# Attention fillers by a fixed count per head instead of a round robin

## The chip, the cores and the metric

The kernel runs on one core of one Trainium2 chip. The metric is the device time of one execution in microseconds (us), taken as the median of several runs. A core has a matrix engine (TensorE, PE in the profile, with PEld for its weight loads), a vector engine (VectorE, DVE), an activation engine (ScalarE, ACT), a general engine (GpSimd, POOL) and a queue that issues the transfers (SyncE, SP). Each engine takes its own instructions strictly in the order in which they stand in the program, and waits for the others on semaphores.

## The reference, cut to what matters

One inference step of two layers on 512 prompt tokens and 8 samples of 4 new tokens each, 544 token columns in all, model width 1024, in fp32. Layer 0 is RWKV-7 time mixing. Layer 1 is native sparse attention (NSA) with 16 query heads on 4 key/value heads:

```python
q, kc, vc, ks, vs, kw, vw, z, gl = jnp.split(h @ w_in, cuts, axis=-1)
...
o = g[..., 0:1] * o_c + g[..., 1:2] * o_s + g[..., 2:3] * o_w    # compressed, selected, window branch
...
return (o.reshape(B, T, NSA_QDIM) * jax.nn.silu(z)) @ w_o
```

So layer 1 is an input projection (28 blocks of 128 output channels), three attention branches for the prompt, the same for the samples against their caches, a gate by silu(z), and an output projection with a residual. The outputs are the new activations, the new key and value rows and the recurrent state.

## The kernel before, in words

Layer 0 is not touched. Layer 1 (`layer1`) is written as Python generators, each of which issues instructions up to its next `yield`; the code at the end of `layer1` decides in what order they are advanced.

* `dense(...)` (`jobs`) does the 28 input projections. One job multiplies a 128-channel weight block, split in two parts for fp32 accuracy, with all 544 columns: 48 matmuls of 128x272 (line 325), 24 into each of two PSUM banks. It yields 8 times, so one dense step is 6 matmuls. In the middle of the next job it does the follow-up of the last one (`post`): head norms (lines 1506 to 1516), key, value and query rows, or the silu of z.
* `attend(k)` goes through the four blocks of 128 queries of key/value head k, in the order of `BO`. A block is done in two halves m (two query heads each). A half computes scores on PE (line 1725), adds the bias table and takes the row maximum on DVE (1752), exponentiates on ACT (1759) and scales the probabilities on DVE or POOL (1779). `attend` yields four times per block, 16 times per head. At each step it also advances the value generator of the block before (`self.pending`): PE transposes (1803), copies from PSUM by ACT (1806) or DVE (1808), value products (1816, 1819), an eviction on ACT (1821) and a store to the DRAM tensor dO (1826). `flush()` advances the values of a head's last block and has four steps of its own.
* `attend_sample(i)` does the samples for the heads 2i and 2i+1, with 32 yields: cache loads and scores (1876, 1884), evictions with bias (1881 to 1892), a softmax (DVE 1896 to 1906, ACT 1901, POOL 1909), transposes (1917 to 1922) and value products (1930 to 1950).
* `gated` loads the stored attention output and silu(z) of six 128-channel blocks, multiplies them (1999) and splits each product into two operands (286 on ACT, 287 on DVE); `project_out` (`part`) multiplies these with the output weights, 48 steps of 6 matmuls (325 again). `project_last` adds the two blocks of head 3 (2041).

Dense jobs, sample steps and the output projection are called fillers: `together(main, filler, n)` advances the filler n times after every step of the attention, and `mix` takes one step from each of its fillers in turn. `until(...)` advances the dense jobs alone until given results exist. All these matmuls share the 3 one-bank PSUM buffers `ph` (a projection takes two at a time, a sample step one); scores and transposes use 2 two-bank buffers `pq`.

The order so written isn't the final one. A scheduler places the instructions of each engine by an estimate of when they can start, with the written order as their priority; it can lift a later matmul over one that it thinks would wait. The code before:

```python
until(("kc", 0), ("ks", 0), ("kw", 0), ("q", 0), ("q", 1))
together(attend(0), jobs, PLAN["N"][0])                  # N = (3, 4, 4, 4)
until(("q", 3), *kv(0))
sample = attend_sample(0)
together(attend(1), mix(jobs, sample), PLAN["N"][1])
until(*kv(1), ("q", 7))
```

Of the kernel before, what the change touches and what calls it, by code (L numbers as in the profile page):

```python
# [2 lines left out]

# [22 lines left out]
PLAN = {  # L26
    'F0': 8,
    'ZN': 7,
    'UN': 7,
    'FN': 3,  # L30
    'LAG': 2,
    'SN': 3,
    'FS': 5,
    'VS': (0, 0, 1, 1, 1, 1, 1, 3),
# [15 lines left out]
    'DS': 4,  # L50
    'BO': ((3, 0, 2, 1), (0, 2, 3, 1), (3, 2, 0, 1), (3, 2, 0, 1)),
    'JO': [('kc', 0), ('ks', 0), ('q', 0), ('kw', 0), ('q', 1), ('vs', 0), ('vc', 0), ('vw', 0), ('kc', 1), ('vc', 1), ('q', 2), ('q', 3), ('ks', 1), ('kw', 1), ('q', 4), ('q', 5), ('vs', 1), ('vw', 1), ('q', 6), ('q', 7), ('z', 0), ('z', 1), ('z', 2), ('z', 3), ('z', 4), ('z', 5), ('z', 6), ('z', 7)],
    'N': (3, 4, 4, 4),
    'PT': 1,
    'PO': 2,
    'PW': 1,
# [17 lines left out]
NR = 32  # L74
F0, ZN, UN, FN, LAG, SN, FS, VS, IV = (PLAN["F0"], PLAN["ZN"], PLAN["UN"], PLAN["FN"], PLAN["LAG"], PLAN["SN"], PLAN["FS"], PLAN["VS"], PLAN["IV"])
TW = 528

VECS = ["nw0", "nw1", "mr", "mw", "mk", "mv", "ma", "mg", "w0", "a0", "kk", "ka", "rk", "lw", "lb"]
VI = {n: i for i, n in enumerate(VECS)}
# [144 lines left out]
class K:  # L224
# [1297 lines left out]
    def layer1(self):  # L1522
# [178 lines left out]
        def kv(i):  # L1701
            return [(n, i) for n in ("kc", "vc", "ks", "vs", "kw", "vw")]

        def bias_tables(k):
            t = self.t("tb", (128, 4, TW))
            for a in range(0, 128, NR):
# [121 lines left out]
        def attend(k):  # L1828

            order = PLAN["BO"][k]  # L1830
            for n, b in enumerate(order):
                if (k, b) not in QZ:
                    stacked_queries(k, b)
                s, v = scores(k, b), self.pending
                next(s)
                if b != order[-1]:
                    stacked_queries(k, order[n + 1])
                next(v, None)
                yield
                for _ in s:  # L1840
                    next(v, None)
                    yield
                for _ in v:
                    yield
                self.pending = values(k, b)
# [3 lines left out]
        def flush():  # L1849
            yield from self.pending  # L1850
            self.pending = iter(())
# [116 lines left out]
        jobs = dense(PLAN["JO"])  # L1968

        def until(*names):  # L1970
            while not ready.issuperset(names):
                next(jobs)

        def together(main, filler, n):
            for _ in main:
                for _ in range(n):
                    next(filler, None)

        def project_out(ks, src, dst):

# [61 lines left out]
                        nc.vector.tensor_tensor(x[:, a], pt[a][:, :HN], x[:, a], OP.add)  # L2042
                    nc.sync.dma_start(O["y"][:, m:m + 2, c], x)

        def mix(*fillers):

            fillers = list(fillers)
            while fillers:
                for f in list(fillers):
                    if next(f, f) is f:  # L2050
                        fillers.remove(f)
                    else:
                        yield

        until(("kc", 0), ("ks", 0), ("kw", 0), ("q", 0), ("q", 1))
        together(attend(0), jobs, PLAN["N"][0])
        until(("q", 3), *kv(0))
        sample = attend_sample(0)
        together(attend(1), mix(jobs, sample), PLAN["N"][1])
        until(*kv(1), ("q", 7))  # L2060
        for _ in sample:
            pass
        sample = attend_sample(1)
        together(attend(2), mix(jobs, sample), PLAN["N"][2])
        together(flush(), mix(jobs, sample), PLAN["N"][2])
        for _ in jobs:
            pass
        for _ in sample:
# [1 line left out]
        gated(range(6))  # L2070
        gate_last()
        part = project_out(range(6), self.dx1, dx2)
        together(attend(3), part, PLAN["N"][3])
        together(flush(), part, PLAN["N"][3])
        for _ in part:
            pass
        project_last()
# [52 lines left out]
```

## Time and profile before

| what | value |
|---|---|
| median of 3 runs | 1046.39 us (1042.59 to 1049.2) |
| the profiled execution's own time | 1041.69 us |
| its span, first to last instruction | 1039.9 us |
| mean granted PE clock | 0.963 of full speed |
| PE busy | 956.3 us, 92% of the span |
| DVE, ACT, POOL busy | 662.8, 566.4, 471.4 us |
| first and last scores of layer 1 (line 1725) | start at 650.2 and 1015.8 us |

In a timeline row stand the start in us, the length in us, the engine, the line, the operation, the tile written and the tile read, and in brackets how long the engine was idle before it and who ended the wait. A stage row gives the stretch, its length, each engine's busy time with its number of instructions, the granted PE clock, the share of the transfer engines and GB/s. Consecutive matmuls overlap, so a row of n matmuls is worth less than n times the mean.

### The profile page before, as it was taken

The page shows a single profiled execution, that of the slowest core. Times are in us where ns is not written, and L with a number is a line of the kernel's source. Part 1 is how long each engine was busy: PE and PEld are TensorE (multiplying, and loading weights), DVE is VectorE, ACT ScalarE, POOL GpSimd, SP SyncE. Part 2 cuts the span into 40 slices and gives each one's busy share as a digit, 9 for nine tenths or more (in the row PEclk, how much of TensorE's full clock was granted, in tenths as well). Part 3 has the DMA queues.
Part 4 walks back from the last instruction along what each step waited for, and adds up shares of the span by engine and source line. Part 5 has one row for each costly group of instructions (what it writes and reads, how often), then busy time and mean ns, then how long its engine had stood idle before and what let it go on. Part 6 is the DMA issues. An engine that isn't in the chain of part 4 may idle for free. (4 is left out here: it accounts for less than half of the span.)

```text
span 1039.9 us, 24788 instructions
## 1 busy us (share of the span) xinstructions
PE 956.3 (92%) x9429; PEld 848.9 (82%) x9429; DVE 662.8 (64%) x1504; ACT 566.4 (54%) x1333; POOL 471.4 (45%) x573
## 2 busy tenths in 40 slices
PE   5799998989989999999898899999799998998997
PEld 4789997979777878888788888998678877896986
DVE  3788578698486542556866724756676557447654
ACT  4357686555444244545544645656675576566452
POOL 5924557755920453312322665755244445244530
PEclk8799999999999999999999989999999998999999
DMA  5685525648654463745684623333435432438543
GB/s 187 198 259 202 166 87 159 195 135 238 195 149 122 139 176 118 225 119 132 155 246 142 228 83 116 104 112 102 113 92 145 120 91 76 129 89 262 168 143 108
DMA packets 151368, 156.69 MB, mean 151 GB/s; under 512 B 53330, under 2 KB 99954, under 8 KB 150994
## 3 DMA queue, kind: packets, MB, share of 16 engines
q1 hardware_dynamic: 151250, 155.11, 50.0%
q8 instruction: 74, 1.21, 0.5%
q14 instruction: 44, 0.36, 0.1%
HBM read 111.33 MB, written 43.93 MB: 149 GB/s over the span
## 5 line engine op out<-in xcount | busy, mean ns | idle before, releaser
L325 PE MATMUL ph<-x,l 128*128 128x272 f32 x2448 | 361.8, 299 | 11.1 <-DVE l L287 2.5
L325 PEld LDWEIGHTS ph<-x,l 128*128 128x128 f32 x2448 | 327.4, 193 | 31.3 <-issue 8.9
L287 POOL TENSOR_TENSOR l<-w,l 128x512 fp32r<-128x512 f32 (+2 forms) x118 | 157.3, 1345 | 128.5 <-ACT l L286 104.8
L286 ACT ACTIVATE l<-w 128x512 fp32r<-128x512 f32 (+2 forms) x160 | 93.9, 613 | 108.5 <-PE ph L325 42.7
L325 PE MATMUL pp<-x,l 128*128 128x272 f32 x768 | 111.8, 300 | 6.0 <-POOL l L287 6.0
L325 PEld LDWEIGHTS pp<-x,l 128*128 128x128 f32 x768 | 104.0, 195 | 8.6 <-POOL l L287 6.2
L1759 ACT ACTIVATE a<-a,st 128x512 f32<-128x512 f32 (+3 forms) x128 | 70.6, 553 | 24.2 <-DVE st L1752 23.8
L1752 DVE CUSTOM_DVE_ANT_0 a<-pq,tb 128x512 f32<-128x512 f32 (+3 forms) x128 | 56.7, 485 | 18.0 <-PE pq L1725 17.8
L1725 PE MATMUL pq<-p,z 128*128 128x512 f32 (+7 forms) x288 | 58.8, 333 | 5.8 <-DVE st L1752 3.2
L1803 PE MATMUL pq<-cst,a 128*128 128x128 f32 x320 | 52.2, 286 | 5.7 <-DVE h L1808 2.9
L1779 DVE TENSOR_SCALAR a<-a,st 128x128 f32<-128x128 f32 (+3 forms) x112 | 56.2, 562 | 0.6
L325 PE MATMUL pp<-t,l 128*128 128x272 f32 x384 | 54.1, 292 | 0.0
L1725 PEld LDWEIGHTS pq<-p,z 128*128 128x128 f32 x288 | 43.4, 193 | 13.1 <-issue 5.1
L325 PEld LDWEIGHTS pp<-t,l 128*128 128x128 f32 x384 | 50.2, 188 | 0.7
L287 POOL TENSOR_TENSOR d<-d,d 128x544 fp32r<-128x544 f32 (+2 forms) x21 | 27.4, 1303 | 51.1 <-ACT d L286 46.7
L1803 PEld LDWEIGHTS pq<-cst,a 128*128 128x128 f32 x320 | 38.4, 145 | 12.7 <-issue 5.0
L1499 DVE TENSOR_TENSOR d<-ph,RS 128x272 f32<-128x272 f32 x56 | 23.9, 436 | 38.7 <-PE ph L325 34.8
L1806 ACT ACTIVATE h<-pq 128x512 f32<-128x512 f32 x60 | 35.3, 589 | 20.9 <-PE pq L1803 19.8
L287 DVE TENSOR_TENSOR l<-w,l 128x512 fp32r<-128x512 f32 x42 | 36.2, 873 | 16.0 <-ACT l L286 14.6
L1819 PE MATMUL pw<-h,p 128*64 128x256 f32 x320 | 40.4, 402 | 2.8 <-ACT h L1806 2.6
L1772 POOL TENSOR_TENSOR cc<-cc,st 128x64 f32<-128x64 f32 x32 | 12.5, 391 | 53.2 <-DVE st L1769 31.2
L666 POOL TENSOR_TENSOR d<-d,d 128x544 f32<-128x544 f32 x8 | 11.0, 1380 | 56.2 <-ACT d L384 56.2
(419 smaller groups left out, 2001.7 us busy)
## 6 DMA issues: line engine op xcount, KB each, us to landing
w<-in_rkvz SPq DMA_DIRECT2D x64, 256.0 KB, 2.8
d<-dram SPq DMA_DIRECT2D x54, 272.0 KB, 3.8
w<-in_win SPq DMA_DIRECT2D x56, 256.0 KB, 3.0
dram<-d SPq DMA_DIRECT2D x48, 272.0 KB, 3.2
ab<-dram SPq DMA_DIRECT2D x32, 256.0 KB, 3.8
p<-in_xT SPq DMA_DIRECT2D x16, 272.0 KB, 3.8
tb<-dram SPq DMA_DIRECT2D x16, 264.0 KB, 7.0
dram<-uar SPq DMA_DIRECT2D x8, 512.0 KB, 3.5
```

Source lines behind the costliest of these rows:

```text
L286: nc.scalar.activation(hi, raw, AF.Copy)
L287: (eng or nc.gpsimd).tensor_tensor(lo, raw, hi.bitcast(F32), OP.subtract)
L325: nc.tensor.matmul((pt[h][:m, :HN] if split else pt[:m, h, :HN]), a[:, k, :m], b[:, h * HN:(h + 1) * HN], start=(k == 0 and n == 0), stop= ...
L1499: self.nc.vector.tensor_tensor(o, p, r, OP.mult)
L1725: nc.tensor.matmul(p[:, par], QZ[k, b][x][:, par, m], kk[:, lo:hi], start=(x == 0), stop=(x == 1))
L1752: nc.vector.tensor_tensor_reduce(out=P[par][j], in0=p[:, par, :n], in1=TB[k][:, g, o:o + n], scale=-1.0, scalar=3.0e38, op0=OP.add, op1=OP ...
L1759: nc.scalar.activation(P[par][j], P[par][j], AF.Exp, scale=-1.0, bias=st[:, 0, g, j + 1:j + 2], accum_out=st[:, 1, g, j + 1:j + 2])
L1772: nc.gpsimd.tensor_tensor(cc[:, gs], cc[:, gs], r[:, :, 0:1].to_broadcast([128, 2, 32]), OP.mult)
L1779: (nc.gpsimd if e == "p" else nc.vector).tensor_scalar(pj, pj, rr, None, op0=OP.mult)
L1803: nc.tensor.transpose(pt[:, g % 2, g // 2], PB[g][j][:, c * 128:c * 128 + 128], ident)
L1806: nc.scalar.activation(w, pt, AF.Copy)
L1819: nc.tensor.matmul(po[r], v, W[x][:, par], start=False, stop=(x == 0), skip_group_check=True)
```

## The change

`mix` and the table `N` go. `paced(main, (filler, total), ...)` advances each filler on its own: after step n of the attention it takes so many steps that total x n / 16 of them (rounded down) are done. A step count of 16 is one head; where `flush` follows in the same chain, its four steps count on at the same rate.

```diff
-        def together(main, filler, n):
+        def paced(main, *fillers):
+
+            n = 0
             for _ in main:
-                for _ in range(n):
-                    next(filler, None)
+                n += 1
+                for f, total in fillers:
+                    for _ in range(total * n // STEPS - total * (n - 1) // STEPS):
+                        next(f, None)
...
         until(("kc", 0), ("ks", 0), ("kw", 0), ("q", 0), ("q", 1))
-        together(attend(0), jobs, PLAN["N"][0])
+        paced(attend(0), (jobs, 56))
         until(("q", 3), *kv(0))
         sample = attend_sample(0)
-        together(attend(1), mix(jobs, sample), PLAN["N"][1])
+        paced(attend(1), (jobs, 48), (sample, 36))
         until(*kv(1), ("q", 7))
         for _ in sample:
             pass
         sample = attend_sample(1)
-        together(attend(2), mix(jobs, sample), PLAN["N"][2])
-        together(flush(), mix(jobs, sample), PLAN["N"][2])
+        paced(chain(attend(2), flush()), (jobs, 60), (sample, 36))
         for _ in jobs:
             pass
...
         part = project_out(range(6), self.dx1, dx2)
-        together(attend(3), part, PLAN["N"][3])
-        together(flush(), part, PLAN["N"][3])
+        paced(chain(attend(3), flush()), (part, 48))
```

In steps of the written order: head 0 takes 56 dense steps instead of 48, head 1 takes 48 instead of 32, head 2 takes all that are left (60 are offered) within its own 16 steps instead of 32 there, 16 beside its flush and the rest alone. The sample steps go from 2 to 2.25 per attention step. The output projection beside head 3 goes from 4 to 3 per step.

The final order on the engines, at three places. Names with numbers are buffers; in the changed file the same statement has another line number (325 is 326, 1725 is 1726, 1803 is 1804, 1816 is 1817, 1819 is 1820, 1876 is 1877; 1999 is 2004, 287 is 288).

First, PE where head 2's first scores (the last of them, 128x32) meet the value products of head 1's last but one block. Before:

```order
L1725 MATMUL pq_1889_11207<-p_1679_9969,z_1884_11188 128x32
L1725 MATMUL pq_1889_11207<-p_1679_9969,z_1885_11189 128x32
L1511 MATMUL ph_1880_11165<-d_1879_11162,mean_480 128x272
L1819 MATMUL pw_1840_10877<-h_1831_10838,p_1526_9062 64x256 x2
L1819 MATMUL pw_1840_10877<-h_1830_10832,p_1526_9062 64x256 x2
L1819 MATMUL pw_1840_10877<-h_1827_10789,p_1526_9062 64x256 x2
L1819 MATMUL pw_1840_10877<-h_1826_10783,p_1526_9062 64x256 x2
```

The same place now:

```order
L1726 MATMUL pq_1889_11207<-p_1659_9857,z_1885_11189 128x32
L326 MATMUL ph_1930_11449<-x_1337_7963,l_1927_11440 128x272
L326 MATMUL ph_1930_11449<-x_1344_7991,l_1926_11439 128x272
L326 MATMUL ph_1930_11449<-x_1345_7992,l_1926_11439 128x272
L326 MATMUL ph_1930_11449<-x_1344_7991,l_1927_11440 128x272
L326 MATMUL ph_1930_11449<-x_1351_8019,l_1926_11439 128x272
L326 MATMUL ph_1930_11449<-x_1352_8020,l_1926_11439 128x272
L326 MATMUL ph_1930_11449<-x_1351_8019,l_1927_11440 128x272
L1877 MATMUL ph_1902_11275<-s_1922_11406,QB1_8192 32x256 x2
L1877 MATMUL ph_1902_11275<-s_1923_11411,QB1_8192 32x256 x2
```

Where one head-norm matmul stood between the scores and the value products, 17 dense matmuls and the samples' scores stand now (ten more dense ones follow these rows, and then the value products).

Second, PE in the flush of head 2, where the last probabilities are transposed (1803). Before, ph is the bank of a dense job:

```order
L325 MATMUL ph_2081_12415<-x_1309_7851,l_2077_12405 128x272
L325 MATMUL ph_2081_12415<-x_1310_7852,l_2077_12405 128x272
L325 MATMUL ph_2081_12415<-x_1309_7851,l_2078_12406 128x272
L1803 MATMUL pq_2063_12286<-cst_63,a_2022_11999 128x128
L1803 MATMUL pq_2063_12286<-cst_63,a_2023_12000 128x128
L1803 MATMUL pq_2063_12286<-cst_63,a_2040_12099 128x128
L1803 MATMUL pq_2063_12286<-cst_63,a_2041_12100 128x128
L325 MATMUL ph_2081_12415<-x_1316_7879,l_2077_12405 128x272
L325 MATMUL ph_2081_12415<-x_1317_7880,l_2077_12405 128x272
L325 MATMUL ph_2081_12415<-x_1316_7879,l_2078_12406 128x272
```

Now (x_2101 and x_2100 are gated operands of the output projection):

```order
L326 MATMUL ph_2147_12709<-x_2101_12513,l_2143_12699 128x272
L326 MATMUL ph_2147_12709<-x_2100_12512,l_2144_12700 128x272
L1804 MATMUL pq_2078_12438<-cst_63,a_2066_12318 128x128
L1804 MATMUL pq_2081_12451<-cst_63,a_2066_12318 128x128
L1804 MATMUL pq_2078_12438<-cst_63,a_2067_12319 128x128
L1817 MATMUL pw_2084_12464<-ct_2077_12436,VM_8196 64x128 x4
L1804 MATMUL pq_2081_12451<-cst_63,a_2067_12319 128x128
L1804 MATMUL pq_2078_12438<-cst_63,a_2047_12197 128x128
L1804 MATMUL pq_2078_12438<-cst_63,a_2048_12198 128x128
```

From the last scores of head 2 to the first of head 3, 123 dense matmuls stood on PE before. Now 33 matmuls of the output projection stand there, and no dense one.

Third, DVE at the gate of the output projection (1999 multiplies, 287 makes the second operand). Before, after the first scores of head 3:

```order
L1752 ISA st_2119_12571 128x1
L1767 TENSOR_SCALAR st_2119_12571<-st_2119_12571 128x6
L1999 TENSOR_TENSOR d_2094_12498<-d_2094_12498,d_2095_12500 128x544
L287 TENSOR_TENSOR x_2089_12486<-d_2086_12480,x_2088_12485 128x544
L1588 TENSOR_TENSOR z_2164_12825<-q_1864_11077,z_2164_12825 64x256 x2
L1746 TENSOR_TENSOR cc_2157_12803<-pq_2158_12804,CB_8198 128x64
```

Now, ahead of the last scaling of head 2's probabilities (1780, before 1779):

```order
L288 TENSOR_TENSOR x_2093_12495<-d_2090_12489,x_2092_12494 128x544
L1768 TENSOR_SCALAR st_2043_12184<-st_2043_12184 128x6
L2004 TENSOR_TENSOR d_2098_12507<-d_2098_12507,d_2099_12509 128x544
L1769 RECIPROCAL st_2043_12184<-st_2043_12184 128x6
L288 TENSOR_TENSOR x_2097_12504<-d_2094_12498,x_2096_12503 128x544
L1770 TENSOR_TENSOR st_2043_12184<-st_2043_12184,GT_8168 128x6
L288 TENSOR_TENSOR x_2101_12513<-d_2098_12507,x_2100_12512 128x544
L1780 TENSOR_SCALAR a_2066_12318<-a_2066_12318,st_2043_12184 128x256 x2
L1780 TENSOR_SCALAR a_2067_12319<-a_2067_12319,st_2043_12184 128x256 x2
```

Four of the six gate products and their splits have moved from behind head 3's first scores to ahead of the end of head 2; the other two stay behind them.

More of the change, by code (lines that the diff above doesn't have):

```diff
@@ L2 @@
 from contextlib import ExitStack
+from itertools import chain
 import numpy as np
@@ L52 @@
     'JO': [('kc', 0), ('ks', 0), ('q', 0), ('kw', 0), ('q', 1), ('vs', 0), ('vc', 0), ('vw', 0), ('kc', 1), ('vc', 1), ('q', 2), ('q', 3), ('ks', 1), ('kw', 1), ('q', 4), ('q', 5), ('vs', 1), ('vw', 1), ('q', 6), ('q', 7), ('z', 0), ('z', 1), ('z', 2), ('z', 3), ('z', 4), ('z', 5), ('z', 6), ('z', 7)],
-    'N': (3, 4, 4, 4),
     'PT': 1,
@@ L76 @@
 TW = 528
+STEPS = 16
 VECS = ["nw0", "nw1", "mr", "mw", "mk", "mv", "ma", "mg", "w0", "a0", "kk", "ka", "rk", "lw", "lb"]
@@ L2043, in project_last @@
                     nc.sync.dma_start(O["y"][:, m:m + 2, c], x)
[L2045 to L2053, printed above, removed]
         until(("kc", 0), ("ks", 0), ("kw", 0), ("q", 0), ("q", 1))
-        together(attend(0), jobs, PLAN["N"][0])
+        paced(attend(0), (jobs, 56))
         until(("q", 3), *kv(0))
         sample = attend_sample(0)
-        together(attend(1), mix(jobs, sample), PLAN["N"][1])
+        paced(attend(1), (jobs, 48), (sample, 36))
         until(*kv(1), ("q", 7))
```

## The prediction

> **What bounds the kernel now.** I read the page first, then the stages of layer 1 from its first attention scores to the end, then the rows of PE in which it waited, and last what DVE did at those places.
>
> The page says which engine carries the work and what one dense matmul is worth:
>
> ```profile
> PE 956.3 (92%) x9429; PEld 848.9 (82%) x9429; DVE 662.8 (64%) x1504; ACT 566.4 (54%) x1333; POOL 471.4 (45%) x573
> ...
> L325 PE MATMUL ph<-x,l 128*128 128x272 f32 x2448 | 361.8, 299 | 11.1 <-DVE l L287 2.5
> ...
> L287 POOL TENSOR_TENSOR l<-w,l 128x512 fp32r<-128x512 f32 (+2 forms) x118 | 157.3, 1345 | 128.5 <-ACT l L286 104.8
> ```
>
> PE is busy for 92% of the span, so an order of the same instructions can only win back time in which PE waits or runs at a lower clock. A dense matmul costs 361.8/2448 = 0.148 us, a dense step of six 0.89 us, and a dense job brings two weight subtractions of 1.35 us on POOL.
>
> Where the waiting is, by stages (length, then PE, PEld, DVE, ACT, POOL busy, then the granted clock):
>
> ```profile
> 713.00:780.00 67.00, 59.30 (x436) 48.02 (x436) 48.48 (x176) 47.67 (x149) 22.40 (x35) 0.95 0.39 105
> 780.00:840.00 60.00, 56.87 (x470) 49.35 (x471) 31.56 (x92) 31.33 (x80) 27.32 (x35) 0.97 0.46 124
> 840.00:885.00 45.00, 40.13 (x288) 34.14 (x287) 32.06 (x91) 33.63 (x95) 22.13 (x25) 0.89 0.30 85
> 885.00:915.00 30.00, 30.00 (x279) 24.10 (x278) 16.75 (x65) 18.24 (x53) 10.02 (x13) 1.00 0.41 121
> 915.00:971.00 56.00, 51.27 (x364) 44.55 (x363) 34.43 (x106) 31.61 (x82) 23.99 (x25) 0.97 0.60 185
> 971.00:1040.00 69.00, 62.34 (x500) 54.98 (x498) 38.28 (x142) 30.35 (x89) 18.36 (x24) 0.99 0.43 136
> ```
>
> From 713 to 885 us PE is idle for 7.7 + 3.1 + 4.9 = 15.7 us. From 885 to 915 it never waits, and from 915 to 971 it loses 4.7 us. The last stage loses 6.7 us, but from the value products of head 3's second block on, its order on PE is the same after the change, so I take it as unchanged. About 20 us, and some clock, are therefore what this change can touch: at most 2% of the time.
>
> **The change part by part.** No instruction is added or removed; the terms are five places on PE.
>
> *1. The start of the samples beside heads 0 and 1 (731 to 760 us).* These are the rows of PE with the waits, and two rows of DVE and POOL that explain the first:
>
> ```profile
> 731.15 3.19 DVE L1779 TENSOR_SCALAR a<-a,st 128x256 f32<-128x256 f32 x4
> 731.62 2.58 POOL L287 TENSOR_TENSOR l<-w,l 128x512 fp32r<-128x512 f32 x2
> ...
> 735.00 0.82 PE L1511 MATMUL ph<-d,mean 128*128 128x272 f32 x2 [2.50 <-DVE s L1881]
> ...
> 747.72 1.11 PE L1725 MATMUL pq<-p,z 128*128 128x160 f32 x8 [1.33 <-DVE st L1752]
> ...
> 750.58 0.41 PE L1803 MATMUL pq<-cst,a 128*128 128x128 f32 x2 [1.28 <-DVE st L1767]
> ...
> 757.25 0.44 PE L1917 MATMUL ph<-cst,s 128*128 128x128 f32 x2 [1.14 <-POOL s L1909]
> ```
>
> ```profile
> 735.00:738.00 3.00, 3.00 (x18) 2.12 (x18) 1.26 (x2) 0.49 (x1) 0.00 (x0) 0.50 0.32 101
> ```
>
> The waits sum to 6.25 us, and the 3 us at half clock after the first cost another 1.5 us: 7.75 us. Between the compressed-value products (line 1621) and the samples' first transposes (1917) only 24 dense matmuls stand on PE, 3.6 us of cover; in the new order 120 stand there, 17.8 us. That covers the last three waits (3.75 us). The first is held by a bank of ph and by scalings that ran beside POOL, and the new order has no dense matmul at that point either; I count 1.25 us of its 4.0. Term: +5 us, ends +1 and +7.75.
>
> *2. Head 1 into head 2 (831 to 844 us).*
>
> ```profile
> 833.61 5.36 PE L1819 MATMUL pw<-h,p 128*64 128x256 f32 x32 [1.89 <-ACT h L1806]
> 843.09 0.86 PE L1876 MATMUL ph<-s,QB 128*32 128x256 f32 x8 [0.69 <-POOL QB L1661]
> ```
>
> Waits of 2.6 us; the 32 value matmuls took 5.36 us, against 3.60 us for the same 32 elsewhere:
>
> ```profile
> 990.53 3.60 PE pw L1819 x32
> ```
>
> So 4.3 us are lost. The first place of the order shows 17 dense matmuls (2.5 us) in front of these value products now. Term: +3.5 us, ends +2 and +4.3.
>
> *3. The samples' second softmax beside head 2 (868 to 882 us).*
>
> ```profile
> 871.30 1.11 PE L1803 MATMUL pq<-cst,a 128*128 128x128 f32 x4 [2.32 <-DVE h L1808]
> ...
> 875.16 1.62 PE L1725 MATMUL pq<-p,z 128*128 128x384 f32 x4 [1.36 <-DVE st L1755]
> ```
>
> ```profile
> 872.00:880.00 8.00, 6.13 (x22) 4.67 (x22) 5.93 (x18) 7.11 (x21) 5.01 (x7) 0.50 0.12 33
> ```
>
> Waits of 3.7 us, and 6.13 us of matmuls at half clock, which is 3.1 us more than at full: 6.8 us. Between the samples' last scores (1884) and their transposes 12 dense matmuls stand before, 30 now, 2.7 us more cover. ACT is busy for 7.11 of these 8 us, so the softmax itself gets no shorter; what is late next is ACT. Term: +4 us, ends +1 and +6.8.
>
> *4. A new bare stretch beside head 1.* In the new order the samples' first transposes stand among scores, transposes and value products of head 1, with no dense matmul from there to head 1's third block. The nearest stages of before, with and without dense cover in the same work:
>
> ```profile
> 744.50:757.30 12.80, 8.79 (x69) 6.57 (x68) 10.95 (x52) 11.79 (x48) 3.96 (x8) 1.00 0.55 116
> 757.30:780.00 22.70, 21.75 (x152) 18.35 (x153) 16.14 (x68) 16.09 (x49) 9.07 (x18) 0.92 0.33 91
> ```
>
> They lose 4.0 and 1.0 us. The new stretch is the barer kind: term -3 us, ends 0 and -5.
>
> *5. The end of head 2 and the gate.* Here the change takes cover away. Before, DVE is nearly free while PE works through the last dense jobs, and then full:
>
> ```profile
> 921.15 1.18 DVE L1779 TENSOR_SCALAR a<-a,st 128x256 f32<-128x256 f32 x4
> ...
> 924.23 0.44 DVE L1499 TENSOR_TENSOR d<-ph,RS 128x272 f32<-128x272 f32 x1 [1.89 <-PE ph L325]
> 927.86 0.44 DVE L1499 TENSOR_TENSOR d<-ph,RS 128x272 f32<-128x272 f32 x1 [3.19 <-PE ph L325]
> ...
> 932.01 0.44 DVE L1499 TENSOR_TENSOR d<-ph,RS 128x272 f32<-128x272 f32 x1 [3.11 <-PE ph L325]
> 935.54 0.44 DVE L1499 TENSOR_TENSOR d<-ph,RS 128x272 f32<-128x272 f32 x1 [3.09 <-PE ph L325]
> 940.53 0.44 DVE L1499 TENSOR_TENSOR d<-ph,RS 128x272 f32<-128x272 f32 x1 [4.55 <-PE ph L325]
> ```
>
> ```profile
> 917.80:961.00 43.20, 38.82 (x270) 33.25 (x269) 25.64 (x82) 26.92 (x67) 16.84 (x16) 0.96 0.59 185
> 941.00:961.00 20.00, 15.62 (x79) 12.35 (x79) 19.16 (x62) 15.95 (x43) 9.21 (x9) 0.91 0.92 299
> ```
>
> From head 2's last scores (917.8) to where the output projection runs freely (961) PE loses 43.2 - 38.8 = 4.4 us. Without the 123 dense matmuls (18.2 us) PE has 20.6 us of work left there, and DVE 25.6 less six evictions of 0.44, or 23.0. If nothing else binds, DVE makes the stretch 23.0 us, and PE loses 2.4: a gain of 2 us against 4.4. This is the one end; that four gate products move into DVE's idle time, as the third place shows, speaks for it.
>
> The other end is the chain. The gate of blocks 4 and 5 needs the values of the last block through DRAM, and two buffered passes on DVE and ACT:
>
> ```profile
> L1821 ACT ACTIVATE h<-pw 128x256 f32<-128x256 f32 x16 | 6.1, 380 | 28.7 <-PE pw L1819 28.7
> ...
> L286 ACT ACTIVATE x<-d 128x544 fp32r<-128x544 f32 x30 | 19.4, 667 | 5.8 <-DVE d L453 2.4 <-DMA d<-dram 1.7 <-PE s L1089 1.1
> ```
>
> ```profile
> L287 DVE TENSOR_TENSOR x<-d,x 128x544 fp32r<-128x544 f32 x6 | 4.7, 779 | 0.0
> L1999 DVE TENSOR_TENSOR d<-d,d 128x544 f32<-128x544 f32 x6 | 4.4, 734 | 0.0
> ```
>
> ```profile
> d<-dram SPq DMA_DIRECT2D x54, 272.0 KB, 3.8
> ...
> dram<-h SPq DMA_DIRECT2D x12, 128.0 KB, 2.7
> ```
>
> That is 0.38 + 2.7 + 3.8 + 0.73 + 0.67 + 0.78 = 9.1 us from the last value product to the operands, where PE has about 6 us of head 3's first scores to do. Before it, the scaling of head 2's last probabilities stands on DVE behind four gate products and four splits (4 x 1.51 = 6.0 us), and PE behind that scaling has only 33 matmuls (4.9 us) of the output projection, which themselves wait for those gates. Such waits were followed by half clock above. Adding 3 us for the round trip, 3 for the scaling and 2 for the clock to the 2.4, PE loses about 10 us: a cost of 6. If the loads are late too it is 12. Term: -5.5 us, ends +2 and -12.
>
> Head 3 itself (3 steps instead of 4) moves matmuls inside a stretch in which PE is busy anyway; I cost it at nothing, and its cover is the output projection, which now lasts to head 3's last block.
>
> Sum: 5 + 3.5 + 4 - 3 - 5.5 = +4 us won. The profiled execution took 1041.69 us, 1.8 more than its span and 4.7 below the median; it would take 1037.7, and the median 1046.39 becomes 1042.4.
>
> **A page of the Trainium skill against the rows.** In the fences the four scalings of 128x256 took 3.19 us beside two weight subtractions on POOL, and 1.18 us at 921, where no subtraction ran. The Trainium skill, "SBUF — State Buffer", section "Who interferes with whom", says that a tensor_scalar in a two-port mode and a GpSimd instruction lock each other out for the whole instruction; the trace agrees, with 2.0 us for such a meeting. It speaks against this change, since dense jobs carry the subtractions into the attention.
>
> **The rivals.**
>
> *The gaps close and the gate costs nothing.* Terms 1 to 3 at their upper ends, 4 and 5 at about zero: 12 to 19 us, so 1027 to 1034, about 1031. For it: DVE's idle time between 922 and 941 (1.89 + 3.19 + 3.11 + 3.09 + 4.55 = 15.8 us), into which the gates move. Against it: the round trip of 9.1 us. Chance 0.28.
>
> *Meetings of POOL and DVE.* The stretches in which dense jobs run alone shrink: head 2 needs 165 dense steps done, and by the end of head 1 it was 137 in the written order (45 + 12 pumped for head 0's values + 48 + 32) and is 159 (45 + 10 + 56 + 48), so 28 steps alone become 6. Those 22 steps are 2.75 jobs, 5.5 subtractions, 7.4 us of POOL work that now runs beside scalings. If PE pays all of it, 1042.4 + 7.4 = 1050. For it: term 1's first wait. Against it: PE has more cover there. Chance 0.08.
>
> *Slower: the gate holds up DVE.* In the new order the four gate products stand ahead of the last scaling of head 2. If their loads (3.8 us each, behind stores on SP) land after DVE reaches them, DVE waits with the scaling behind it, and with that the transposes, the values, the store, the reload and all six operands. With two load times (7.6 us) and the round trip in full on top of DVE's 23.0 us, the stretch is 39.7 us for 20.6 us of PE work, 14.7 us worse than before; with terms 1 to 3 at 4 us in all, 1046.4 + 10.7 = 1057. It decides from about 4 us of waiting on DVE in front of the gate products. Chance 0.12.
>
> *The change moves nothing.* The scheduler might have restored the old order; the three places exclude it on PE and DVE. Chance 0.02, at 1046.
>
> **How the numbers follow.** The forecast, 1036 to 1047, has the remaining 0.50. Over 1% means more than 10.5 us, which is about what a measurement of this kernel can tell (its three runs lie 6.6 us apart). Faster by that: the first rival and a little of the forecast's edge, 0.30. Slower: the gate rival and a trace of the meetings, 0.13. Same: 0.57. The range from 1029 to 1055 leaves out the best of the first rival and the worst of the gate.
>
> **What would show it.** Right: idle time of PE in the stretch of the samples' start (now 7.7 us) at half or less; no wait ahead of head 1's value products for its third block; about 10 us lost between head 2's last scores and the free output projection, with waits on gate operands (line 288, formerly 287) and at half clock. Wrong: a transition with less than 5 us lost (then the first rival), or DVE waiting for loads ahead of its gate products (then the slower one), or new waits on scalings stretched by POOL in head 1.

## The result, and the profile after

The changed kernel took 1032.72 us in the median of 4 runs (1030.77 to 1035.79) beside 1044.49 us for the kernel before: a ratio of 0.990 with a 95% interval from 0.986 to 0.994. Run once more beside other kernels it gave 0.991 (0.987 to 0.995). It is faster by about 1%, 9 to 12 us; the forecast was a gain of 4 us, to 1042.4, so the sign was right and the size too small by 5 to 8 us. Its profiled execution took 1032.77 us with a span of 1031.0, against 1041.69 and 1039.9.

The page of the changed kernel, engines and dense matmuls (its line numbers are one above those of before):

```profile
PE 949.3 (92%) x9429; PEld 845.1 (82%) x9429; DVE 666.8 (65%) x1504; ACT 565.8 (55%) x1333; POOL 474.3 (46%) x573
...
L326 PE MATMUL ph<-x,l 128*128 128x272 f32 x2448 | 362.6, 299 | 13.4 <-ACT x L287 4.0 <-DVE l L288 2.4 <-DVE d L348 1.3
```

The same 9429 matmuls keep PE busy for 7.0 us less. About 5 of them are time at half clock, by the clock of the stage rows below (11.1 us before, 6.0 after).

To compare kernels whose layer 0 ends at different times, I cut layer 1 from its first scores on (650.2 us before, 650.9 after) into five places: A, 60 to 150 us later, the samples' start beside heads 0 and 1; B, 150 to 200, head 1 into head 2; C, 200 to 255, the samples' second softmax; D, 255 to 320, the end of head 2 and the gate; E, 320 to 360, the middle of head 3. First the stages of before, then those of after (length, PE, PEld, DVE, ACT and POOL busy, granted clock, DMA share, GB/s):

```profile
710.20:800.20 90.00, 82.30 (x646) 67.03 (x643) 59.67 (x207) 60.53 (x181) 32.68 (x49) 0.96 0.40 108
800.20:850.20 50.00, 46.18 (x356) 39.85 (x355) 26.89 (x80) 28.36 (x73) 22.64 (x29) 0.97 0.42 109
850.20:905.20 55.00, 50.81 (x407) 42.58 (x406) 34.18 (x112) 36.02 (x107) 23.01 (x27) 0.91 0.36 105
905.20:970.20 65.00, 60.27 (x444) 51.66 (x443) 42.41 (x129) 38.33 (x98) 30.02 (x31) 0.97 0.55 171
970.20:1010.20 40.00, 39.17 (x315) 36.10 (x315) 22.88 (x86) 21.07 (x60) 17.28 (x21) 1.00 0.47 148
```

```profile
710.90:800.90 90.00, 86.08 (x699) 73.26 (x696) 63.73 (x209) 62.94 (x184) 38.66 (x55) 0.98 0.41 112
800.90:850.90 50.00, 49.19 (x404) 42.47 (x404) 29.33 (x83) 31.71 (x80) 25.20 (x29) 1.00 0.52 140
850.90:905.90 55.00, 51.67 (x424) 44.80 (x423) 31.26 (x106) 34.60 (x99) 25.56 (x29) 0.97 0.35 105
905.90:970.90 65.00, 55.19 (x395) 45.90 (x393) 47.36 (x151) 40.60 (x117) 25.75 (x30) 0.95 0.57 172
970.90:1010.90 40.00, 39.26 (x324) 34.59 (x322) 23.13 (x99) 19.72 (x63) 13.76 (x18) 1.00 0.40 125
```

What PE loses in a stage is its idle time plus the part of its busy time that the clock took: length - busy + busy x (1 - clock). For A before that is 7.70 + 82.30 x 0.04 = 11.0 us. The loss in us:

| | A | B | C | D | E | sum |
|---|---|---|---|---|---|---|
| before | 11.0 | 5.2 | 8.8 | 6.5 | 0.8 | 32.3 |
| after | 5.6 | 0.8 | 4.9 | 12.6 | 0.7 | 24.6 |

So A, B and C win 13.7 us, D gives 6.1 back, and 7.7 are left. From the first scores to the end of the span the kernel went from 389.7 to 380.1 us, 9.6 less; the remaining 1.9 lie outside the five losses (the clock in a row has two decimals, which alone is 0.4 us in a stage of 82).

PE's waits in the changed kernel, places A to D:

```profile
728.42 0.39 PE L1512 MATMUL ph<-d,mean 128*128 128x272 f32 x1 [0.94 <-POOL d L288]
731.38 0.73 PE L1512 MATMUL ph<-d,mean 128*128 128x272 f32 x2 [1.20 <-ACT d L1514]
732.36 1.12 PE L1817 MATMUL pw<-ct,VM 128*64 128x128 f32 x8 [0.25 <-ACT VM L1624]
767.42 0.94 PE L1726 MATMUL pq<-p,z 128*128 128x384 f32 x4 [1.50 <-DVE st L1756]
...
805.05 0.44 PE L1958 MATMUL ph<-cst,s 128*128 128x128 f32 x2 [0.48 <-ACT s L1955]
...
869.92 0.66 PE L1804 MATMUL pq<-cst,a 128*128 128x128 f32 x4 [0.57 <-DVE h L1809]
...
876.77 0.63 PE L1804 MATMUL pq<-cst,a 128*128 128x128 f32 x4 [1.75 <-DVE st L1756]
...
919.28 0.30 PE L1792 MATMUL pw<-cst,cc 128*128 128x128 f32 x1 [1.31 <-ACT h L1822]
921.46 0.64 PE L326 MATMUL ph<-x,l 128*128 128x272 f32 x3 [1.13 <-ACT x L287]
...
946.37 0.92 PE L326 MATMUL ph<-x,l 128*128 128x272 f32 x3 [2.83 <-ACT x L287]
948.58 1.08 PE L1804 MATMUL pq<-cst,a 128*128 128x128 f32 x4 [1.29 <-DVE a L1780]
```

The wait for the first head norm is still there, as two (0.94 and 1.20). The three waits behind it are gone, one new one stands at 767 us. The wait ahead of head 1's value products (1.89 us before) is gone. The longest of all now stands in D, 2.83 us for an operand of the gate; D has two more over 1 us at 919 and 921, the first for the eviction of head 2's values, the second for a gate operand as well.

### The profile page after: what moved, and what is told of

The parts are those of the page before. It is cut to its first block, busy times and chain, and to the rows that moved or that the text cites. A ratio compares the mean times of both kernels' runs of the same rounds, so it can differ in the third digit from the quotient of the medians.

```text
span 1031.0 us, 24779 instructions
## 1 busy us (share of the span) xinstructions
PE 949.3 (92%) x9429; PEld 845.1 (82%) x9429; DVE 666.8 (65%) x1504; ACT 565.8 (55%) x1333; POOL 474.3 (46%) x573
## 4 chain that ended last, share of the span: by engine, by line
PE 46%; DVE 11%; DMA 6%; POOL 4%; ACT 4%; issue 3%; SPq 1%; DVEq 0%; POOLq 0%; ACTq 0%
PE ph L326 21%; PE pq L1726 3%; PE pw L1820 3%; PE pq L1804 2%; POOL l L288 2%; PE pr L1156 2%; DMA d<-dram 2%; PE ph L2046 1%; ACT a L1760 1%; DVE a L1780 1%; DVE l L288 1%; ACT l L287 1%; PE ph L371 1%; DMA out_swkv<-p 1%; DVE a L1753 1%
## 5 line engine op out<-in xcount | busy, mean ns | idle before, releaser
L1804 PE MATMUL pq<-cst,a 128*128 128x128 f32 x320 | 49.5, 278 | 3.7 <-DVE st L1756 1.8
L1780 DVE TENSOR_SCALAR a<-a,st 128x128 f32<-128x128 f32 (+3 forms) x112 | 50.9, 514 | 0.5
L1773 POOL TENSOR_TENSOR cc<-cc,st 128x64 f32<-128x64 f32 x32 | 12.6, 395 | 52.7 <-DVE st L1770 43.5
```

Source lines behind the costliest of these rows:

```text
L1780: (nc.gpsimd if e == "p" else nc.vector).tensor_scalar(pj, pj, rr, None, op0=OP.mult)
L1804: nc.tensor.transpose(pt[:, g % 2, g // 2], PB[g][j][:, c * 128:c * 128 + 128], ident)
```

## The experiments

My first theory was that cover for heads 0 and 1 makes the gain, while head 2's cover and its gate cancel. The rival: the gain sits in head 2. The first four kernels are the kernel before with one or two heads changed; the fillers of the other heads stay a round robin. Here is what all twelve gave: the ratio to the kernel before, the layer-1 length from first scores to the end of the span in the profiled execution, and the losses there. Lengths carry less scatter than whole times: the first scores, ahead of which all these programs have the same order on PE, start anywhere from 650.2 to 657.1 us. But each row is one execution, and where two kernels have the same order one can see how far two executions differ inside layer 1. The two profiles of the whole change have the same order throughout and are 0.2 us apart at the end. The kernel before and head 3 alone have the same order on PE for the first 316 us after the first scores and are 0.8 us apart there. Heads 0, 1, 2 and the whole have it for 307 us and are 3.8 us apart there, nearly all of it in D. So a difference of 4 us in D between two rows isn't yet an effect of the edit.

| kernel | ratio (95% interval) | layer 1, us | A | B | C | D | E |
|---|---|---|---|---|---|---|---|
| before | 1 | 389.7 | 11.0 | 5.2 | 8.8 | 6.5 | 0.8 |
| head 0 alone | 0.996 (0.993 to 0.999) | 385.0 | 10.2 | 0.5 | 3.3 | 8.6 | 2.7 |
| head 1 alone | 1.000 (0.998 to 1.003) | 388.0 | 6.0 | 0.5 | 6.2 | 11.7 | 6.5 |
| heads 0, 1 | 1.000 (0.997 to 1.003) | 386.6 | 5.6 | 4.9 | 5.7 | 8.9 | 3.2 |
| head 2 alone | 1.007 (1.003 to 1.010) | 395.2 | 11.1 | 4.7 | 3.1 | 8.6 | 6.2 |
| head 3 alone | 0.999 (0.996 to 1.002) | 389.4 | 11.1 | 5.1 | 8.8 | 7.3 | 0.4 |
| heads 0, 1, 2 | 0.996 (0.993 to 0.999) | 386.5 | 5.9 | 0.8 | 4.9 | 16.3 | 2.6 |
| heads 0, 1, 3 | 0.996 (0.994 to 0.999) | 384.4 | 5.9 | 4.9 | 5.9 | 8.9 | 1.1 |
| whole, again | 0.991 (0.987 to 0.995) | 379.9 | 5.9 | 0.8 | 4.9 | 12.0 | 0.5 |
| cover in the flush | 0.990 (0.987 to 0.993) | 377.3 | 4.1 | 0.8 | 7.8 | 8.4 | 0.5 |
| gate freed | 0.986 (0.982 to 0.989) | 372.4 | 5.7 | 0.8 | 4.9 | 2.5 | 4.0 |
| other amounts | 0.989 (0.986 to 0.992) | 377.9 | 5.0 | 0.4 | 4.9 | 11.1 | 0.6 |
| last values direct | 0.991 (0.987 to 0.994) | 378.0 | 5.9 | 0.8 | 4.9 | 12.0 | 0.9 |

### Heads 0 and 1 together

```diff
-        together(attend(0), jobs, PLAN["N"][0])
+        paced(attend(0), (jobs, 56))
-        together(attend(1), mix(jobs, sample), PLAN["N"][1])
+        paced(attend(1), (jobs, 48), (sample, 36))
```

> Heads 0 and 1 alone get the new amounts (56 dense steps; 48 dense and 36 sample steps), heads 2 and 3 keep the round robin. Theory (the gain is the cover of heads 0 and 1, head 2's change is about neutral): 10 to 14 us under the kernel before, so 0.987 to 0.990, about the time of the whole change; PE's half-clock stretches of 730 to 840 us shrink to one, and the transition from head 2 to head 3 still loses about 4 us. Rival (the gain is head 2's even spread and the earlier gate): 0 to 4 us under it, 0.996 to 1.000. My prediction's own terms 1, 2 and 4 make 5.5 us.

1045.14 us against 1043.99: no gain, where 10 to 14 us were expected. A closes (5.6), but B stays open (4.9), with another wait than before. This kernel's lines stand two above those of before; line 1653 evicts a result of a dense job:

```profile
828.52 0.66 PE L1818 MATMUL pw<-ct,VM 128*64 128x128 f32 x8 [2.37 <-ACT VN L1653]
```

With only 6 dense steps alone ahead of head 2 and the old round robin behind them, the value products come before that result. E grew too, from 0.8 to 3.2. The theory fell here. This kernel's profiled execution (1041.66 us) is among its fastest, so its length of 386.6 may be some 3 us too good; why its other executions took longer isn't shown by one trace.

### Head 2 alone

```diff
-        together(attend(2), mix(jobs, sample), PLAN["N"][2])
-        together(flush(), mix(jobs, sample), PLAN["N"][2])
+        paced(chain(attend(2), flush()), (jobs, 60), (sample, 36))
```

> Head 2 alone gets the new amounts (60 dense and 36 sample steps in its sixteen attention steps, nothing left for the flush). Theory (cover of the samples' second softmax against the gate's round trip): within 3 us of the kernel before, 0.997 to 1.003, with about 10 us of PE lost between head 2's last scores and the free output projection, and no half-clock stretch at the samples' second softmax. Rival (the gain sits in head 2): 8 to 12 us under it, 0.989 to 0.992. The prediction's terms 3 and 5 make +1.5 us of loss.

1050.69 us, 0.65% slower: both theories missed, since neither made it slower by 7 us. C closes as forecast (8.8 to 3.1) and D costs 2 more, but the loss is in E, which the change of head 2 doesn't touch in the written order:

```profile
977.10:1017.10 40.00, 35.20 (x274) 31.85 (x273) 17.68 (x65) 16.21 (x47) 13.16 (x16) 0.96 0.42 133
```

Head 3's value products for its second block wait 3.04 us for a copy on ACT there and then run at half clock; the kernel with head 1 alone, below, shows why.

### Head 0 alone, and head 1 alone

Each is one half of the first diff.

> Head 0 alone gets 56 dense steps instead of 48. If the samples' start was bare because head 0 had too few dense steps, the stretch of 731 to 760 us of before closes here and the run is 3 to 8 us under the kernel before (0.992 to 0.997); if the order inside head 1 made it bare, within 1.5 us of it.

1039.35 us, 4.6 less, but not where expected: A goes only from 11.0 to 10.2. The gain is in B (5.2 to 0.5) and C (8.8 to 3.3).

> Head 1 alone gets 48 dense and 36 sample steps instead of a round robin of 64. Theory: the 16 dense steps more inside head 1, and the sample finished inside it, take 6 to 10 us off the kernel before (0.990 to 0.994), more than head 0 alone. Rival (head 0 decides): within 2 us of the kernel before.

1044.15 us, no gain. A closes here (6.0), B closes too, and the win is given back in D (11.7) and E (6.5). So A is head 1's: its 48 dense steps and the sample spread over all sixteen steps. And here too E is worse although nothing after head 1 is written in another order. Where head 3's second block has its value products, SP, ACT and PE of this kernel (a row of SP shows when it issues a transfer; line 298 loads a weight, 288 splits it, 1808 copies transposes from PSUM, 2000 stores a result of the output projection):

```profile
985.36 0.33 SPq L2000 DMA_DIRECT2D dram<-d  x1
985.78 0.87 SPq L298 DMA_DIRECT2D w<-in_nwo  x2
...
989.78 0.52 ACT L288 ACTIVATE l<-w 128x384 fp32r<-128x384 f32 x1 [6.34 <-DMA w<-in_nwo]
991.66 0.52 ACT L288 ACTIVATE l<-w 128x384 fp32r<-128x384 f32 x1 [1.36 <-DMA w<-in_nwo]
992.09 0.58 ACT L1808 ACTIVATE h<-pq 128x512 f32<-128x512 f32 x1
...
992.72 5.36 PE L1821 MATMUL pw<-h,p 128*64 128x256 f32 x32 [3.06 <-ACT h L1808]
```

The two loads of the next output weight stand on SP behind a store that can't go before its result is evicted; SP waits 4.7 us for DVE there. ACT waits 6.34 and 1.36 us for them with the copy behind it in its queue, and PE waits for that copy. This wait of 3.06 us and the half clock behind it (1.4 us) are 4.5 of E's 6.5 us here; the other 2.1 are waits further on, which the kernel without head 3 shows below. With head 2 alone changed the same pair is there (6.33 and 1.32 us). In the kernel before ACT waits for the same weights at other moments, and its copies aren't behind:

```profile
986.10 0.53 ACT L286 ACTIVATE l<-w 128x384 fp32r<-128x384 f32 x1 [1.08 <-DMA w<-in_nwo]
986.99 0.60 ACT L1806 ACTIVATE h<-pq 128x512 f32<-128x512 f32 x1 [0.37 <-PE pq L1803]
```

### Head 3 alone

```diff
-        together(attend(3), part, PLAN["N"][3])
-        together(flush(), part, PLAN["N"][3])
+        paced(chain(attend(3), flush()), (part, 48))
```

> Head 3 alone gets the new amount (48 steps of the output projection over sixteen attention steps and its flush, so three a step instead of four). New theory, after heads 0 and 1 together gave nothing and head 2 alone was 7 us slower: the gain of the whole change needs head 3. If head 3 is worth the gain by itself, 6 to 12 us under the kernel before (0.988 to 0.994). If it only saves what head 2's change spoils, within 2 us of it (0.998 to 1.002). My prediction costed head 3 at nothing.

1042.94 against 1042.16, ratio 0.999: by itself head 3 is worth nothing. A to C are as before to 0.1 us, and E goes from 0.8 to 0.4, since there was nothing to win.

### All but head 3, and all but head 2

> The whole change without head 3: heads 0, 1 and 2 with the new amounts, head 3 with four steps of the output projection after each attention step as before. If head 3 is what is missing, 3 to 8 us slower than the kernel before (1.003 to 1.008; the sum of heads 0 and 1 and of head 2 measured apart is +6.7), with bare value products at half clock in head 3. If the parts only interact among heads 0 to 2, 8 to 12 us faster (0.988 to 0.992), like the whole.

1040.92 us, ratio 0.996: neither 3 to 8 us slower nor as fast as the whole, although the two intervals touch (0.993 to 0.999 against 0.987 to 0.995). Places A to C are those of the whole change (5.9, 0.8, 4.9); what is missing is D (16.3 against 12.0) and E (2.6 against 0.5), 6.4 us together. Only E can be put down to head 3's amount. In D the two kernels have the same order on PE up to 307 us after the first scores, and on DVE, ACT and POOL still longer, and this execution is 3.8 us later there already. In it DVE waits 1.80 us for a load of the gate where the whole change waited 1.13 us in its second profile and not at all in its first, and half clock costs 6.0 us in D against 2.8. Whether that is chance one execution of each can't tell; the twelve executions of this kernel spread from 1031.4 to 1044.7 us.

In E the output projection has run out. With four of its steps after each attention step its last matmul of this part (line 327 here) comes at 1003 us, and the scores of head 3's third block behind it (1727) wait with nothing beside them:

```profile
1002.99 0.87 PE L327 MATMUL ph<-x,l 128*128 128x272 f32 x5
...
1006.66 0.71 PE L1727 MATMUL pq<-p,z 128*128 128x256 f32 x4 [1.09 <-DVE st L1757]
```

Three more waits of 0.74, 0.23 and 0.58 us follow, 2.64 in all, which is E's loss. With three steps 19 matmuls of the output projection stand right before these scores, and there is no wait. The kernels with head 1 alone and with heads 0 and 1, which have four steps too, lose the same way there (1.09, 0.74 or 0.75, 0.23).

> The whole change without head 2: heads 0, 1 and 3 with the new amounts. If head 2's amounts are a loss of about 7 us wherever they stand, this is faster than the whole change, 14 to 18 us under the kernel before (0.983 to 0.987). If head 2 and head 3 belong together (head 2's earlier end is made good only by head 3's thinner cover), 0 to 6 us under it (0.994 to 1.000).

1040.29 us, ratio 0.996. Without head 2, B stays open (4.9 against 0.8) and C is 1.0 worse, while D is 3.1 better. So head 2 isn't a loss wherever it stands: beside the other three edits it wins 4.5 us of layer 1 (384.4 to 379.9), and alone it costs 7.

> The changed kernel once more, beside the others on the same chip, since its first comparison has few runs: 8 to 12 us under the kernel before (0.988 to 0.992) by every theory.

1032.99 us, ratio 0.991, as expected. Its layer 1 took 379.9 us, against 380.1 in the first profile, while its first scores started 3.7 us later.

The four parts measured alone make, of 1043 us, -4.5 + 0.5 + 6.8 - 1.3 = +1.5 us, each with an interval of some 3 us either way; the whole makes -9.8. The parts do not add, so no head owns the gain.

### Other amounts

```diff
-        paced(attend(0), (jobs, 56))
+        paced(attend(0), (jobs, 52))
-        paced(attend(1), (jobs, 48), (sample, 36))
+        paced(attend(1), (jobs, 52), (sample, 36))
```

> The changed kernel with 52 dense steps in each of heads 0 and 1, instead of 56 and 48; the sum is the same, so head 2 starts from the same state. If even amounts as such close the gaps, within 3 us of the whole change (0.988 to 0.993). If the exact numbers happen to suit the scheduler's order, 4 to 10 us slower than it (0.995 to 1.000).

1032.6 us, ratio 0.989. The losses are those of the second profile of the whole change within 1 us in each place. The gain doesn't hang on 56 and 48.

### Cover in the flush of head 2

```diff
-        paced(chain(attend(2), flush()), (jobs, 60), (sample, 36))
+        paced(chain(attend(2), flush()), (jobs, 48), (sample, 36))
```

> The changed kernel with 48 dense steps spread over head 2's sixteen attention steps and three more in each of the flush's four, so twelve of them cover head 2's last values, instead of 60 in the attention and a bare flush. If the bare flush costs what the transition from head 2 to head 3 lost (12.1 us in waits and half clock, 6.1 before), 3 to 6 us faster than the whole change (0.984 to 0.988 of the kernel before). If the round trip of the last values costs it, which the cover only delays, within 2 us of the whole change (0.989 to 0.992); and if three dense steps instead of 3.75 open the samples' second softmax again, 2 to 4 us slower than it (0.992 to 0.995).

1031.8 us, ratio 0.990: not told apart from the whole change. The stages say why; C and D of this kernel:

```profile
851.30:906.30 55.00, 50.17 (x404) 41.81 (x403) 32.60 (x110) 33.97 (x104) 22.59 (x28) 0.94 0.33 98
906.30:971.30 65.00, 59.55 (x431) 52.71 (x430) 47.37 (x147) 40.12 (x110) 29.17 (x33) 0.95 0.57 180
```

D falls from 12.0 to 8.4, C rises from 4.9 to 7.8. (A, ahead of the edit, is lower too, by half clock that didn't occur; see the end.) By these rows both readings were right at once: the bare flush costs up to 4 us (no more than two executions of one order differ by in D), and the cover for it is taken from the samples' second softmax.

### The gate freed from head 2's values

```diff
-                nc.sync.dma_start(o, dO[:, m])
+                nc.sync.dma_start(o, dO[:, m % 4])
```

> The changed kernel with the loads for the gate of blocks 4 and 5 taken from blocks 0 and 1 of the stored attention output, so that no gate product waits for head 2's last values to go through memory. This changes the computation: channel blocks 4 and 5 of the gated output hold head 0's values instead of head 2's. If the round trip (8.9 us from the last value product to the first operand in the trace) makes the waits of the transition, 4 to 7 us faster than the whole change (0.983 to 0.987). If the work that piles up on DVE and ACT there makes them, within 2 us of it (0.989 to 0.992).

1026.95 us, ratio 0.986. Against the whole change's 12.0 or 12.6, D loses 2.5 us:

```profile
906.90:971.90 65.00, 62.46 (x486) 55.56 (x485) 48.85 (x151) 41.61 (x117) 30.09 (x35) 1.00 0.65 204
```

486 matmuls fit into these 65 us, where the changed kernel did 395, and the clock is full, with DVE no less busy (48.9 against 47.4 us). So not DVE's or ACT's work costs D its time, but waiting for head 2's last values. E takes 3.5 of the gain: less of the output projection is left for it, and the waits of head 3's third block are back (1.09, 0.43, 0.24 and 0.58 us).

### The last values gated without the way through memory

The run before can mean two things: the way through memory is long, or the output projection, which is the only cover left, can't start before the values exist. In the changed kernel the way is this; rows of PE, ACT, SP, DVE, ACT and PE:

```profile
935.51 1.95 PE L1820 MATMUL pw<-h,p 128*64 128x256 f32 x16
937.78 0.36 ACT L1822 ACTIVATE h<-pw 128x256 f32<-128x256 f32 x1
938.16 0.38 SPq L1827 DMA_DIRECT2D dram<-h  x1
940.92 0.42 SPq L2001 DMA_DIRECT2D d<-dram  x1
944.84 0.72 DVE L2004 TENSOR_TENSOR d<-d,d 128x544 f32<-128x544 f32 x1
945.68 0.64 ACT L287 ACTIVATE x<-d 128x544 fp32r<-128x544 f32 x1
946.37 0.92 PE L326 MATMUL ph<-x,l 128*128 128x272 f32 x3 [2.83 <-ACT x L287]
```

From the end of the value products to the first product with the gated operand: 946.37 - 937.46 = 8.9 us. The next kernel keeps the computation, but gates these 128 tokens from the evicted tile; it loads and multiplies the other tokens in two pieces:

```diff
-            if k == 3:
+            if k == 2 and b == PLAN["BO"][2][-1]:
+                self.late = ok, tk
+            elif k == 3:
...
+                    c = slice(tk, tk + 128)
+                    nc.vector.tensor_tensor(o[:, c], ok[:, m - 4], z[:, c], OP.mult)
```

> The changed kernel, correct, with head 2's last block of values (tokens 128 to 255 of channel blocks 4 and 5) gated straight from its evicted tile instead of being stored and loaded again; the other tokens are loaded as before. The round trip of the last values is gone, four more multiplications of a part of the columns stand on DVE. If the round trip alone makes the transition's loss, about the time of the run without the wait, 4 to 7 us under the whole change (0.983 to 0.987 of the kernel before). If the loads behind it on SP or DVE's work hold the gate as well, within 2 us of the whole change (0.989 to 0.992).

1035.3 us, ratio 0.991, the same as the whole change. The way is short now:

```profile
942.53 3.09 PE L1820 MATMUL pw<-h,p 128*64 128x256 f32 x16
945.68 0.39 ACT L1822 ACTIVATE h<-pw 128x256 f32<-128x256 f32 x1 [0.78 <-PE pw L1820]
946.10 0.49 DVE L2017 TENSOR_TENSOR d<-h,d 128x128 f32<-128x128 f32 x2 [2.01 <-ACT h L1822]
946.42 1.21 ACT L287 ACTIVATE x<-d 128x544 fp32r<-128x544 f32 x2 [0.36 <-DVE d L2017]
947.51 0.54 PE L326 MATMUL ph<-x,l 128*128 128x272 f32 x3
...
953.61 0.55 DVE L1753 CUSTOM_DVE_ANT_0 a<-pq,tb 128x384 f32<-128x384 f32 x1
954.94 0.43 DVE L1995 TENSOR_TENSOR d<-ph,d 128x272 f32<-128x272 f32 x1
955.42 4.79 PE L326 MATMUL ph<-x,l 128*128 128x272 f32 x25 [2.58 <-DVE d L1995]
```

947.51 - 945.62 = 1.9 us instead of 8.9. But the values themselves come later. The products end 290.2 us after the first scores, against 286.6 in the changed kernel, so the operands are there only 3.4 us earlier, not 7. Part of the reason stands on DVE: the gate products of the other tokens (2015) are now ahead of a copy (1809) of head 2's last transposes, and wait for their loads:

```profile
937.21 0.66 DVE L2015 TENSOR_TENSOR d<-d,d 128x128 f32<-128x128 f32 x2 [3.22 <-DMA d<-dram]
937.78 0.68 DVE L1809 COPY h<-pq 128x512 f32<-128x512 f32 x1
```

In the changed kernel this copy had no load ahead of it; now PE waits 0.62 and 0.92 us behind such DVE work. The 16 value products then take 3.09 us instead of 1.95, at half clock, and a new wait of 2.58 us follows: the output projection's first bank is evicted on DVE (1995) behind head 3's score evictions (1753), and PE waits for the bank. D stays at 12.0, with 1.9 us less of idle time than in the second profile of the whole change and 1.8 more of half clock.

So this run doesn't show what a shorter way alone is worth: it took 7 us off the way behind the values and put a wait for loads ahead of them, which is the second reading of its expectation. Freeing the output projection from these values altogether bought about 10 us in D. Whether the length of the way makes that, or that PE has no other work left, the two runs don't separate. A kernel with both, the direct way and cover in the flush, wasn't run.

## Why the prediction was right or wrong

**Where the time is.** Right: the five places and no others carry the change. By places the forecast was A +2 (terms 1 and 4), B +3.5, C +4, D -5.5, E 0, in sum +4; measured (with the sign of a gain) +5.4, +4.4, +3.9, -6.1, +0.1, in sum +7.7, and 1.9 outside them. The time of 1032.7 lies below the main forecast of 1036 to 1047, near the first rival's 1031.

**Term 1, and term 4 with it: the terms that were mis-sized.** The term was 5 us of "7.75 us", the waits of four rows and one half-clock stretch. The stage row shows that A lost 11.0: there were 1.45 us more of idle time (one wait of 0.58 and short ones) and 1.8 more of half clock, after the later waits as well as the first. I had taken a list of waits for the stage's loss. After the change the first wait with its half clock still costs 0.94 + 1.20 + 0.25 and 1.7 of clock, 4.1 us, against 4.0 before: the 1.25 that I gave it were not won. All the rest went, so term 1 is 11.0 - 4.1 = 6.9 instead of 5. Term 4 was -3 at a price of 4.0 for the barer kind of stretch; it came to a wait of 1.50 without half clock, and 0.48 in B. Together 3.4 us of the 5.6 that the forecast fell short of.

**Term 2** was +3.5 with an end at +4.3, and B won 4.4: both the wait and the half clock went. But the reason was too simple. It isn't only the matmuls that now stand in front: with heads 0 and 1 changed and head 2 not, B lost 4.9 through another wait.

**Term 3**: +4 forecast, +3.9 measured. The wait ahead of the transposes fell from 2.32 to 0.57 us; a later one of 1.75 stayed, as ACT and DVE are what is late next.

**Term 5**: -5.5 forecast as a cost of "about 10 us" of PE time; D's idle time alone is 9.8 us, and with the clock D costs 6.1 more than before. The 9.1 us of the way through memory, added up from rows of before, were 8.9; PE waited 2.83 us for the operand behind it, where 3 had been added, and half clock cost 2.8 instead of 2. The 3 us for the scaling didn't come: no wait stands right ahead of the transposes of head 2's last probabilities at 930. In their place PE waited 1.31, 1.13 and 0.68 us between 918 and 927, for an eviction and for gate operands. So the path was right, and the sum came out right partly by luck: a part that didn't come was made up by waits that it hadn't named. That the waiting for head 2's values is the cost is shown by the kernel with the gate freed (D 2.5).

**Head 3, costed at nothing.** Against the kernel before that is what E shows (0.8 to 0.7). As a statement on the edit it is wrong: with the old four steps beside the other three edits E loses 2.1 us more, because the output projection runs out before head 3's third block. The prediction read head 3 in the order of before, where the projection started later and so lasted. Nor is the order the same from the value products of head 3's second block on, as it says: the changed kernel has 361 matmuls from there to the end, 12 more than before, all of the output projection.

**The rivals.** "The gaps close and the gate costs nothing" named 1031, close to the time, by the wrong way: the gate does cost. "Meetings of POOL and DVE" went the other way. The scalings on DVE, before and after:

```profile
L1779 DVE TENSOR_SCALAR a<-a,st 128x128 f32<-128x128 f32 (+3 forms) x112 | 56.2, 562 | 0.6
```

```profile
L1780 DVE TENSOR_SCALAR a<-a,st 128x128 f32<-128x128 f32 (+3 forms) x112 | 50.9, 514 | 0.5
```

They took 5.3 us less, not more, although more of the dense jobs run inside the attention: 27 of the 112 overlapped a weight subtraction on POOL before, and 19 after. The Trainium skill's rule on the shared port ("SBUF — State Buffer", "Who interferes with whom") fits what a single meeting costs, but it doesn't say how many meetings an order brings, and I had counted subtractions moved instead of meetings. "The gate holds up DVE" needed 4 us of DVE waiting for loads; DVE waited 0.56 in the first profile and at most 1.13 in the second:

```profile
918.85 1.87 DVE L2004 TENSOR_TENSOR d<-d,d 128x544 f32<-128x544 f32 x1 [0.56 <-DMA d<-dram]
```

**What stays open.** E's loss has two causes in the traces: with head 1 or head 2 alone mostly the queue of store, weight load, split and copy, and in the kernels whose output projection is spent early the bare waits of head 3's third block. Why the scheduler lines up the queue so after an edit to an earlier head was not tried, and no run loads the weights early. Why D is 4.3 us worse without head 3 at the same order, and what the 1.9 us outside the five places are, has no cause shown.

## What to carry to other kernels

Price a stage by its idle time plus its clock deficit, from one stage row, before listing waits; the list missed 3.3 of 11.0 us here. A spread of fillers is a property of the whole order: four edits that were worth -4.5, +0.5, +6.8 and -1.3 us alone were worth -9.8 together, and by the traces each leaves a later stage with another amount of cover. And where a chain seems to bind, measure when its end comes, not only how long it is: a way cut from 8.9 to 1.9 us brought its operands only 3.4 us earlier and won nothing that was measured, while the edit put a wait for loads ahead of it. Freeing PE's other work from the chain won 10 us in that stage and 5 in all.

## What the runs showed of the hardware

The clock: the waits alone don't settle whether half clock follows. After the single wait of 1.50 us at 767 the clock stayed at 1.00; after 0.94 and 1.20 within 4 us PE ran at half clock for about 3 us, as it did before after one wait of 2.50. But the kernel with cover in the flush has the same order on PE there and the same waits, 0.94, 1.20 and then 0.47 us, and its clock stayed at 1.00:

```profile
731.80 0.51 PE L1512 MATMUL ph<-d,mean 128*128 128x272 f32 x2 [1.20 <-ACT d L1514]
```

```profile
732.00:736.00 4.00, 3.53 (x39) 2.08 (x39) 3.96 (x10) 3.41 (x9) 1.23 (x2) 1.00 0.43 139
```

The same four microseconds of the changed kernel had a granted clock of 0.64. So two executions of one order can differ by 1.7 us in A through the clock alone. What decides isn't shown here, and a term for the clock has to be read from stage rows, with that much doubt.

Two profiles of the same program differ by 3.7 us in when layer 1 begins and by 0.2 us in how long it takes. Most of the scatter between executions of these two lies ahead of the change.
